# A two-layer attention and expert trunk on one core: paired products, and a branch over the first expert's quads

## The chip, the cores and the metric

The kernel runs on one core of a Trainium2 chip. The core has TensorE (PE, with its weight loads PEld), VectorE (DVE), ScalarE (ACT), GpSimd (POOL) and SyncE (SP), and 16 DMA engines. TensorE runs at one of two clock levels, 1.2 or 2.4 GHz; the profile gives the granted clock as a share of the higher. The metric is the device time of one execution in microseconds, by the median of several runs.

## The reference

256 tokens of width 1024 pass two layers, each an attention and a feed-forward part with a layer norm behind it. Layer 0 has sliding-window attention (16 heads) and a dense SwiGLU of 3584. Layer 1 has attention in three branches (compressed keys and values, selected blocks, window) and eight SwiGLU experts of 3584, of which each token takes two.

```python
def reference(x, ...):
    cos, sin = _rope_tables(x.shape[1])
    for i in range(DEPTH):
        j = i // 2
        if i % 2 == 0:
            h = _swa_sink_attention(x, a_w_in[j], a_w_out[j], a_sinks[j], cos, sin)
        else:
            h = _nsa_attention(x, b_w_in[j], b_w_out[j], b_cmp_pos_k[j], b_cmp_pos_v[j],
                               b_cmp_k_w1[j], b_cmp_k_w2[j], b_cmp_v_w1[j], b_cmp_v_w2[j], cos, sin)
        x = _layer_norm(DN_ALPHA * x + h, ln_gain[i, 0], ln_bias[i, 0])
        if i % 2 == 0:
            f = _swiglu(x, ffn_w_gate[j], ffn_w_up[j], ffn_w_down[j])
        else:
            f = _moe(x, moe_router[j], moe_w_gate[j], moe_w_up[j], moe_w_down[j])
        x = _layer_norm(DN_ALPHA * x + f, ln_gain[i, 1], ln_bias[i, 1])
    return x

# inside _nsa_attention
    def compress(t, pos, w1, w2):
        blk = t[:, idx] + pos[None, None, :, None, :]
        flat = blk.transpose(0, 1, 3, 2, 4).reshape(B, nc, Hkv, CMP_LEN * HEAD_DIM)
        return jax.nn.gelu(flat @ w1) @ w2
    kcc = compress(kc, pos_k, ck_w1, ck_w2)
    vcc = compress(vc, pos_v, cv_w1, cv_w2)

def _moe(x, router, w_gate, w_up, w_down):
    xt = x.reshape(B * S, D)
    logits = (xt @ router).astype(jnp.float32)
    vals, ids = lax.top_k(logits, TOP_K)
    w = jax.nn.softmax(vals, axis=-1)
    gate = jnp.sum(jax.nn.one_hot(ids, N_EXPERTS, dtype=jnp.float32) * w[..., None], axis=1)
    for e in range(N_EXPERTS):
        out = out + gate[:, e:e + 1].astype(xt.dtype) * _swiglu(xt, w_gate[e], w_up[e], w_down[e])
```

## The kernel before

**Stages.** Everything is one unrolled program. `plan` lists the weights in the order of use as tiles of 1 MB (2048 columns of 128 partitions), and `load` asks for them on SP's queue (L168) as soon as a buffer is free: seven `raw` buffers, and in the experts seven `more` and five `later`. The first tile is cut into two pieces. The products of layer 0 and of the projections split each weight tile into `hi` (ACT, L120) and `lo` (DVE, L121) and take three products of 128x512 each (`mm3`, L204 to L206). At the start PE transposes x (L224), ACT and DVE split the transposed tokens into `Th` and `Tl`, and `project` makes the products of token tile 0, then 1.

**Compression.** In `compress` the products of keys and values with `w1` (L803) have 64 columns of PE each: 16 for keys and then 16 for values, both to the same half of the columns (each is two rows in the trace). The sum `hc` is 64 partitions by 512; the gelu (L807 to L815) is a chain of ACT and DVE steps on that shape, then four transposes (L820).

**Attention of layer 1.** `unit(t, j, heads)` does scores, softmax, transposes and value products (L948) of a pair of heads j. For t = 0 both heads are in one unit and the products alternate between the two halves of PE's columns; for t = 1 each head is a unit of its own, with its eight trace rows all in one half. Units are pipelined by `pairs` with one step of each between the products of the last query projection.

**Experts.** Expert 0's gathering (`first_gather`, L1092) is interleaved by hand with the router in a `manual_schedule` of PE, DVE, POOL and ACT. An expert of at most 96 tokens has its first 64 done as *halves* (`halves`, two column halves, L1187 for gate and up, L1210 for down) and the other 32 as *quads* (`quarters`, four column quarters, L1195 and L1216). Expert 0 always has both, as have four other places; three places have 64 only (`CAPS`). `two` does one and then the other and turns the order round each time, so that two groups of the same kind follow each other. An expert has four chunks of 1024, 1024, 1024 and 512, with gate, up and down in each: twelve groups of halves, and twelve of quads. In the experts PE's order is as written. Behind the router, DVE counts and ranks the experts (L1359 to L1366); SP loads seven registers from `whole` (L1381) to know which expert's weights to ask for next, and its queue stands still until it has them. At the end of the program all engines branch over the code for overflowing experts (L1402, L1403).

## Time and profile before

| what | us |
|---|---|
| median of three runs (1411.89 to 1418.05) | 1413.41 |
| the profiled execution | 1413.78 |
| its span | 1412.0 |
| PE busy in the span | 1360.7 (96%) |
| DVE busy | 442.0 (31%) |
| ACT busy | 342.4 (24%) |

The granted clock was 0.99 of the higher level in the mean. The share of PE is high throughout, but PE is busy for two reasons: up to about 530 us because its products are the longest work, and behind that because the experts' products take about as long as the transfer of their weights (434.86 MB in all, 308 GB/s over the span, about 405 in the experts). A row of the timeline gives start and length in us, engine and line, the operation with the tile written and the tiles read, the shape and the count; in brackets stands the idle time before it and who ended it.

### The profile page before, as it was taken

What the parts mean: (1) busy time and instruction counts of PE and PEld (TensorE: products, weight loads), DVE (VectorE), ACT (ScalarE), POOL (GpSimd) and SP (SyncE); (2) the same over time, 40 slices, a digit from 0 to 9 for tenths busy, and PEclk for the clock granted to TensorE, in tenths of its full rate; (3) what the DMA queues carried; (4) which work ended last, traced back from release to release, by engine and by line L of the source; (5) the groups of instructions that cost most, each with busy time, mean ns of one, the idle gap of its engine ahead of it and who ended that gap; (6) DMA issues with size and microseconds to landing.
All of it is one profiled execution on the core that took longest, in us unless ns stands there. A gap on an engine that the chain in (4) does not pass through costs nothing. (4 is left out here: it accounts for less than half of the span.)

```text
span 1412.0 us, 23279 instructions
## 1 busy us (share of the span) xinstructions
PE 1360.7 (96%) x9761; PEld 784.5 (56%) x9762; DVE 442.0 (31%) x1004; ACT 342.4 (24%) x783; POOL 8.4 (1%) x17
## 2 busy tenths in 40 slices
PE   7999999999999999999999999999998999999984
PEld 6777888887777774453344354444343454445331
DVE  6876544556958753000101001100100100200103
ACT  5754444444456721010001001000101000100100
POOL 0000000000000000000000000000000000000000
PEclk9999999999999998999999999999999999999997
DMA  9516565554372067899999999999999999999994
GB/s 349 181 61 211 181 192 192 179 179 155 122 271 91 31 266 272 345 389 377 409 403 409 407 401 409 408 402 407 408 402 409 408 401 408 408 395 393 408 402 179
DMA packets 143679, 434.86 MB, mean 308 GB/s; under 512 B 11312, under 2 KB 18128, under 8 KB 143568
## 3 DMA queue, kind: packets, MB, share of 16 engines
q1 hardware_dynamic: 138416, 428.85, 79.3%
q10 hardware_dynamic: 5152, 4.45, 1.0%
q8 instruction: 79, 1.29, 0.4%
q14 instruction: 32, 0.26, 0.1%
HBM read 432.23 MB, written 1.05 MB: 307 GB/s over the span
## 5 line engine op out<-in xcount | busy, mean ns | idle before, releaser
L121 DVE TENSOR_TENSOR lo<-raw,hi 128x512 fp32r<-128x512 f32 (+2 forms) x244 | 166.4, 730 | 106.5 <-ACT hi L120 106.3
L1187 PE MATMUL ps<-more,Th 128*64 128x512 f32 (+1 forms) x920 | 186.8, 555 | 5.7 <-DMA more<-in_moe_w_gate 5.4
L120 ACT ACTIVATE hi<-raw 128x512 fp32r<-128x512 f32 (+2 forms) x244 | 146.0, 659 | 142.4 <-PE ps L206 129.5
L204 PE MATMUL ps<-hi,Th 128*128 128x512 f32 (+1 forms) x432 | 171.4, 397 | 4.4 <-ACT hi L120 3.2
L206 PE MATMUL ps<-hi,Tl 128*128 128x512 f32 (+1 forms) x432 | 168.6, 391 | 1.4 <-DVE Tl L121 1.4
L205 PE MATMUL ps<-lo,Th 128*128 128x512 f32 (+1 forms) x432 | 168.3, 390 | 0.0
L1244 DVE TENSOR_TENSOR h<-h,ps 128x512 f32<-128x512 f32 (+1 forms) x32 | 19.9, 621 | 448.4 <-PE ps L1187 448.4
L1187 PE MATMUL ps<-later,Th 128*64 128x512 f32 (+1 forms) x680 | 128.9, 525 | 2.1 <-DMA later<-in_moe_w_gate 1.8
L1187 PEld LDWEIGHTS ps<-more,Th 128*64 128x64 f32 x920 | 65.0, 138 | 115.5 <-issue 98.4
L204 PEld LDWEIGHTS ps<-hi,Th 128*128 128x128 f32 x432 | 81.9, 190 | 23.6 <-ACT hi L120 3.6
L1187 PE MATMUL ps<-raw,Th 128*64 128x512 f32 (+1 forms) x448 | 94.4, 561 | 0.6 <-ACT Th L1095 0.6
L1210 PE MATMUL ps<-more,hTa 128*64 128x512 f32 x408 | 92.2, 595 | 2.7 <-DMA more<-in_moe_w_down 2.7
L1236 ACT ACTIVATE h<-ps 128x512 f32<-128x512 f32 (+1 forms) x32 | 17.4, 544 | 315.1 <-PE ps L1187 315.1
L206 PEld LDWEIGHTS ps<-hi,Tl 128*128 128x128 f32 x432 | 81.8, 189 | 20.4 <-DVE Tl L121 2.9
L205 PEld LDWEIGHTS ps<-lo,Th 128*128 128x128 f32 x432 | 82.0, 190 | 16.8 <-DVE lo L121 0.4
L1187 PEld LDWEIGHTS ps<-later,Th 128*64 128x64 f32 x680 | 47.8, 137 | 72.1 <-issue 60.1
L1210 PE MATMUL ps<-later,hTa 128*64 128x512 f32 x312 | 70.3, 594 | 2.0 <-DMA later<-in_moe_w_down 2.0
L1210 PEld LDWEIGHTS ps<-more,hTa 128*64 128x64 f32 x408 | 28.4, 137 | 60.6 <-issue 54.6
L1187 PEld LDWEIGHTS ps<-raw,Th 128*64 128x64 f32 x448 | 31.7, 139 | 53.1 <-issue 48.6
L1195 PE MATMUL ps<-more,Th 128*32 128x256 f32 (+1 forms) x1136 | 60.2, 359 | 0.0
L1239 ACT ACTIVATE hb<-ps 128x256 f32<-128x256 f32 (+1 forms) x20 | 7.2, 358 | 189.0 <-PE ps L1195 189.0
L1243 DVE TENSOR_TENSOR hb<-hb,ps 128x256 f32<-128x256 f32 (+1 forms) x20 | 7.8, 388 | 142.3 <-PE ps L1195 142.3
(256 smaller groups left out, 1444.5 us busy)
## 6 DMA issues: line engine op xcount, KB each, us to landing
more<-in_moe_w_up SPq DMA_DIRECT2D x53, 1024.0 KB, 18.1
more<-in_moe_w_down SPq DMA_DIRECT2D x51, 1024.0 KB, 18.0
more<-in_moe_w_gate SPq DMA_DIRECT2D x50, 1024.0 KB, 18.2
later<-in_moe_w_down SPq DMA_DIRECT2D x38, 1024.0 KB, 15.1
later<-in_moe_w_gate SPq DMA_DIRECT2D x36, 1024.0 KB, 18.3
later<-in_moe_w_up SPq DMA_DIRECT2D x35, 1024.0 KB, 18.0
raw<-in_moe_w_gate SPq DMA_DIRECT2D x26, 1024.0 KB, 18.0
raw<-in_moe_w_up SPq DMA_DIRECT2D x24, 1024.0 KB, 18.2
```

The source lines that it names most:

```text
L120: state["act"] = ACT.activation(hi, src, AF.Copy)
L121: DVE.tensor_tensor(lo, src, hi.bitcast(F32), op=OP.subtract)
L204: PE.matmul(ps, xh, wh, start=first, stop=False)
L205: PE.matmul(ps, xh, wl, start=False, stop=False)
L206: PE.matmul(ps, xl, wh, start=False, stop=last)
L1187: PE.matmul(pa[h * CA:(h + 1) * CA, :wide // 2], T[:, k, :CA], parts[k // n][:, k % n, h * wide // 2:(h + 1) * wide // 2], start=k == 0, s ...
L1195: PE.matmul(pb[q * CB:(q + 1) * CB, :wide // 4].rearrange("p (b f) -> p b f", f=CB), T[:, k, CA:], w[:, q], start=k == 0, stop=k == KT - 1)
L1210: PE.matmul(ya[o * CA:(o + 1) * CA, :], hT[0][:, f % (n // 2), f // (n // 2), :], parts[f // 2][:, f % 2, o * 512:(o + 1) * 512], **ends(f))
L1236: ACT.activation(ha, ga[:, :wide // 2], AF.Silu)
L1239: ACT.activation(hb, gb[:, :wide // 4], AF.Silu)
L1243: DVE.tensor_tensor(hb, hb, ub[:, :wide // 4], op=OP.mult)
L1244: DVE.tensor_tensor(ha, ha, ua[:, :wide // 2], op=OP.mult)
```

## The change

- `zeros` is made first, on DVE, and in a manual schedule PE does seven products with it ahead of the transposes of x and five behind them.
- The first weight tile is cut into four pieces, which are asked for on ACT's queue.
- The tiles of `w1` come in turns for keys and values, and their products go to one half of the columns each, in turns; the gelu runs on 128x256, with two transposes of 128x128.
- The value products of head 0 of token tile 1 are kept and issued with those of head 1, in turns.
- Expert 0 does its halves first each time; a register on PE (`beyond`, the count of expert 0 less 64) decides whether its quads are branched over. The banks that quads would fill are set to zero by DVE. `cnt` and `beyond` are made inside the manual schedule.

The three calls of `gate_up` and `down`, which pass `x`, are left out.

```diff
+    zeros = const.tile([P, P], BF16, name="zeros")
+    DVE.memset(zeros, 0.0)
     cbf = const.tile([P, 3 * P], BF16, name="cbf")
...
             pieces = min(n, pieces if state["loaded"] < len(order) - 2 else 2)
+            queue = ACT if len(order) > 99 and state["loaded"] == 1 else SP
             for k in range(0, n, n // pieces):
-                SP.dma_start(raw[:, k:k + n // pieces, :], src[:, k:k + n // pieces, :])
+                queue.dma_start(raw[:, k:k + n // pieces, :], src[:, k:k + n // pieces, :])
             raws.append((raw, exact, kind))
...
     wa, wo = a["a_w_in"][0], a["a_w_out"][0]
-    plan(wa[:, :512], pieces=2)
+    plan(wa[:, :512], pieces=4)
     for c in (1024, 512):
...
     KC, VC, KS, VS, KW, VW, GL = (1024 + 256 * k for k in range(7))
-    w1s = [a[w][0, q * 1024:(q + 1) * 1024, :] for w in ("b_cmp_k_w1", "b_cmp_v_w1") for q in range(2)]
+    w1s = [a[w][0, q * 1024:(q + 1) * 1024, :] for q in range(2) for w in ("b_cmp_k_w1", "b_cmp_v_w1")]
     plan(wb[:, KC:KC + 512])
...
         with tc.manual_schedule(engines={PE.engine}):
+            idle = bank()
+            def turn_over(n):
+                for _ in range(n):
+                    PE.matmul(idle, zeros, zeros.unsqueeze(1).to_broadcast([P, 4, P]), start=True, stop=True)
+            turn_over(7)
+            Ts[0]
+            turn_over(5)
             for _ in project(Ts, 512, ps_q[0], 2):
...
-    zeros = const.tile([P, P], BF16, name="zeros")
-    POOL.memset(zeros, 0.0)
     SP.dma_start(cmask, a["cmask"].rearrange("(t p) k c -> p t k c", p=P))
...
             DVE.tensor_copy(posT, pb[:, :32].rearrange("p (a b) -> p a b", a=2))
-            hc = bank().rearrange("p (k h) -> p k h", k=2)[:C]
+            hc = bank()[:, :CMP_HID]
             Xs = wts.tile([P, 2, CMP_LEN // 2, NKV, CP], F32, name="X", tag="raw", bufs=RAW)
...
                 yield
-            for k in range(2):
-                for q in range(2):
-                    (r,), = take()
-                    for i in range(8):
-                        PE.matmul(hc[:, k, :], Xs[:, k, q * 8 + i].rearrange("p g c -> p (g c)"), r[:, i, :],
-                                  start=q == 0 and i == 0, stop=q == 1 and i == 7, skip_group_check=True)
+            for q in range(2):
+                r = [w for (w,) in take(2, 1 + q)]
+                for i in range(8):
+                    for k in range(2):
+                        PE.matmul(hc[k * C:(k + 1) * C, :], Xs[:, k, q * 8 + i].rearrange("p g c -> p (g c)"),
+                                  r[k][:, i, :], start=q == 0 and i == 0, stop=q == 1 and i == 7,
+                                  skip_group_check=True)
                 yield
-            hx, hy = (pool.tile([P, 2, CMP_HID], F32, name="hx", tag="pt", bufs=PT)[:C] for _ in range(2))
+            hx, hy = (pool.tile([P, CMP_HID], F32, name="hx", tag="pt", bufs=PT) for _ in range(2))
             ACT.activation(hx, hc, AF.Copy)
...
             yield
-            pb = bank().rearrange("p (k j c) -> p k j c", k=4, j=2)[:, :2, :, :]
-            for k in range(2):
-                for j in range(2):
-                    PE.transpose(pb[:, k, j, :], hx[:, k, j * P:(j + 1) * P], ident[:C, :C])
+            pb = bank()[:, :CMP_HID].rearrange("p (j k c) -> p k j c", j=2, k=2)
+            for j in range(2):
+                PE.transpose(pb[:, :, j, :].rearrange("p k c -> p (k c)"), hx[:, j * P:(j + 1) * P], ident)
...
-        sums = {}
+        sums, waiting = {}, {}
...
             yield
-            if heads[0] == 0:
+            if heads[-1] == 1:
                 sums[t, j] = bank()[:, :P]
-            po = sums[t, j]
-            for m, (i, br, k) in enumerate(steps):
-                h = heads[i]
-                PE.matmul(po[h * HD:(h + 1) * HD, :], v[:, k, br, g, :], pt[:, m * P:(m + 1) * P],
-                          start=k + br == 0, stop=False, skip_group_check=True)
+            po = sums.get((t, j))
+            held = waiting.setdefault((t, j), [])
+            held += [(k, br, heads[i], pt, m) for m, (i, br, k) in enumerate(steps)]
             if heads[-1] == 1:
+                for k, br, h, x, m in sorted(held, key=lambda e: e[:3]):
+                    PE.matmul(po[h * HD:(h + 1) * HD, :], v[:, k, br, g, :], x[:, m * P:(m + 1) * P],
+                              start=k + br == 0, stop=False, skip_group_check=True)
                 PE.matmul(po, vcc[:, j // 4, j % 4].rearrange("p e d -> p (e d)"), pcT[:, t, j // 4, :], start=False,
...
-            self.cap, self.slot, self.gate = cap, slot_e, gate_e
+            self.cap, self.slot, self.gate, self.more, self.ask = cap, slot_e, gate_e, None, None
...
-        def two(first, second, between=None):
+        def two(x, first, second, between=None):
-            steps = [first, second][::-1 if state["turn"] and second else 1]
-            if second:
+            both, ask = second is not None, x.ask is not None
+            steps = [first, second][:1 + both]
+            if both and not ask:
+                if state["turn"]:
+                    steps.reverse()
                 state["turn"] = 1 - state["turn"]
-            steps[0]()
-            if between:
-                between()
-            if second:
-                steps[1]()
+            for i, step in enumerate(steps):
+                if i == 1 and ask:
+                    state["turn"] = 1
+                    x.more = x.ask() if x.more is None else x.more
+                    with tc.If(x.more > 0):
+                        step()
+                else:
+                    step()
+                if i == 0 and between:
+                    between()
-        def gate_up(pa, pb, T, wide):
+        def cleared(ps, x):
+            if x.ask is not None:
+                DVE.memset(ps, 0.0)
+        def gate_up(pa, pb, x, wide):
+            T = x.T
+            if pb is not None:
+                cleared(pb[:, :wide // 4], x)
             parts = [w for (w,) in take(KT * wide // PART, 0)]
...
-            two(halves, pb is not None and quarters)
+            two(x, halves, quarters if pb is not None else None)
-        def down(c, hT, ya, yb, between=None):
+        def down(c, hT, ya, yb, x, between=None):
+            if yb is not None and c == 0:
+                cleared(yb[:, :256], x)
             n = WIDE[c] // P
...
-            two(halves, yb is not None and quarters, between)
+            two(x, halves, quarters if yb is not None else None, between)
...
     mvs = {}
+    cnt = moe.tile([P, NE], F32, name="cnt")
+    beyond = moe.tile([P, 1], I32, name="beyond")
     with tc.manual_schedule(engines={PE.engine, DVE.engine, POOL.engine, ACT.engine}):
...
         next(gathering)
+        ps = bank()[:, :NE]
+        for t in range(NT):
+            PE.matmul(ps, ones, asb[:, t, :], start=t == 0, stop=t == NT - 1)
+        DVE.tensor_copy(cnt, ps)
+        DVE.tensor_scalar(beyond, cnt[:, 0:1], -float(CA), 0.0, op0=OP.add, op1=OP.max)
         for _ in share():
             pass
+    experts[0].ask = lambda: nc.values_load(beyond[0:1, :], engines=[PE.engine], min_val=0, max_val=S)
     halves_pool.__exit__(None, None, None)
...
-    ps = bank()
-    for t in range(NT):
-        PE.matmul(ps[:, :NE], ones, asb[:, t, :], start=t == 0, stop=t == NT - 1)
-    NR = NE - 1
-    cnt, key, rank = (moe.tile([P, NE], F32, name=x) for x in ("cnt", "key", "rank"))
+    key, rank = (moe.tile([P, NE], F32, name=x) for x in ("key", "rank"))
     is_at = moe.tile([P, NE, NE], F32, name="is_at")
...
-    DVE.tensor_copy(cnt, ps[:, :NE])
     DVE.scalar_tensor_tensor(key, cnt, float(NE), iota8, op0=OP.mult, op1=OP.add)
```

The first place is PE in the attention of layer 1: L948 is the value products, L951 the compressed part, L939 transposes, L920 scores. Before, around the second unit of a pair with t = 1:

```order
L948 MATMUL ps<-pt,v 64x128 x4
L206 MATMUL ps<-hi,Tl 128x512
L939 MATMUL ps<-cf,p 128x128 x4
L917 LDWEIGHTS cbf
L917 MATMUL ps<-masks,cbf 128x512
L920 MATMUL ps<-kT,qT_2938 128x256 x4
L948 MATMUL ps<-pt,v 64x128 x4
L951 MATMUL ps<-pcT,vcc 128x128
```

After, where L963 is L948:

```order
L210 MATMUL ps<-hi,Tl 128x512
L951 MATMUL ps<-cf,p 128x128 x4
L929 LDWEIGHTS cbf
L929 MATMUL ps<-masks,cbf 128x512
L932 MATMUL ps<-kT,qT_2955 128x256 x4
L963 MATMUL ps<-pt,v 64x128 x8
L965 MATMUL ps<-pcT,vcc 128x128
```

The first head's products no longer stand with the mask and scores ahead, and eight program rows for both heads stand where the second head's four stood.

The second place is PE at the first expert: L1092 is the gathering, L1187 halves, L1195 quads. Before:

```order
L1092 MATMUL ps<-pick,x_80 128x96 x4
L1187 MATMUL ps<-raw,Th 64x512
L1092 MATMUL ps<-pick,x_80 128x96 x4
L1187 MATMUL ps<-raw,Th 64x512 x15
L1195 MATMUL ps<-raw,Th 32x256 x56
L1195 MATMUL ps<-more,Th 32x256 x8
L1187 MATMUL ps<-raw,Th 64x512 x12
```

After, where L1106 is the gathering, L1218 halves, L1226 quads and L1365 the register:

```order
L1106 MATMUL ps<-pick,x_82 128x96 x8
L1360 LDWEIGHTS cbf
L1360 MATMUL ps<-asb,cbf 128x8
L1360 LDWEIGHTS cbf
L1360 MATMUL ps<-asb,cbf 128x8
L1218 MATMUL ps<-raw,Th 64x512 x16
L1365 TENSOR_LOAD beyond
L1365 ISA x2
L1196 COMPARE_AND_BRANCH
L1226 MATMUL ps<-raw,Th 32x256 x32
L1196 UNCONDITIONAL_BRANCH x2
L1218 MATMUL ps<-raw,Th 64x512 x12
```

All eight gathering products stand ahead of the first halves, the count's products (L1360) follow them, and each group of quads stands between a branch that compares and two that don't.

The third place is DVE behind the router: `w2t` is the softmax of the two choices, `whole` the ranked experts. Before:

```order
L1362 TENSOR_TENSOR tmp<-key 128x64
L1363 TENSOR_REDUCE rank<-tmp 128x8
L1364 TENSOR_TENSOR is_at<-cf,rank 128x64
L1356 TENSOR_TENSOR tmp<-is_at,cf 128x64
L1357 TENSOR_REDUCE numbers<-tmp 128x8
L1366 CAST whole<-numbers 128x8
L1356 TENSOR_TENSOR tmp<-is_at,slot 128x64
L1357 TENSOR_REDUCE slots<-tmp 128x8
L1356 TENSOR_TENSOR tmp<-is_at,slot 128x64
L1075 TENSOR_SCALAR pick<-cf,slots 128x64
L1357 TENSOR_REDUCE slots<-tmp 128x8
L1044 TENSOR_SCALAR w2t<-w2t 128x2
```

After, just behind the first step on `w2t` (L1058):

```order
L1399 TENSOR_TENSOR tmp<-key 128x64
L1059 RECIPROCAL w2t<-w2t 128x2
L1400 TENSOR_REDUCE rank<-tmp 128x8
L1061 TENSOR_TENSOR w2t<-w2t 128x2
L1062 TENSOR_TENSOR hot<-hot,w2t 128x2x8
L1401 TENSOR_TENSOR is_at<-cf,rank 128x64
L1064 TENSOR_TENSOR hot<-hot,w2t 128x2x8
L1394 TENSOR_TENSOR tmp<-is_at,cf 128x64
L1066 TENSOR_TENSOR hot<-hot 128x2x8
L1395 TENSOR_REDUCE numbers<-tmp 128x8
L1068 CAST gates<-hot 128x16
L1403 CAST whole<-numbers 128x8
```

The cast to `whole` stood ahead of the first step on `w2t` behind ACT; now six steps on `w2t`, `hot` and `gates` stand between the ranking's and ahead of the cast. On SP the register loads of `whole` then stand behind one more weight tile. Before:

```order
L168 DMA more<-in_moe_w_gate 128x2x1024 x4
L168 DMA more<-in_moe_w_up 128x2x1024
L168 DMA later<-in_moe_w_up 128x2x1024
L168 DMA more<-in_moe_w_up 128x2x1024
L1381 TENSOR_LOAD whole
L1381 ISA x2
```

After:

```order
L172 DMA more<-in_moe_w_up 128x2x1024
L172 DMA later<-in_moe_w_up 128x2x1024
L172 DMA more<-in_moe_w_up 128x2x1024
L172 DMA later<-in_moe_w_up 128x2x1024
L1418 TENSOR_LOAD whole
L1418 ISA x2
```

The second `later` tile of `in_moe_w_up` has come ahead of the loads.

## Rows read from the trace of the kernel before

**Rows 1.** The page's 40 slices of the span: bandwidth of the transfers in each.

```profile
GB/s 349 181 61 211 181 192 192 179 179 155 122 271 91 31 266 272 345 389 377 409 403 409 407 401 409 408 402 407 408 402 409 408 401 408 408 395 393 408 402 179
```

**Rows 2.** Timeline of SyncE's queue: start, length, instruction, count.

```profile
506.90 0.37 SPq L168 DMA_DIRECT2D more<-in_moe_w_up  x1
...
537.54 0.38 SPq L168 DMA_DIRECT2D later<-in_moe_w_up  x1
```

**Rows 3.** Timeline of TensorE and ScalarE at the start; idle time before in brackets.

```profile
9.39 0.79 PE L204 MATMUL ps<-hi,Th 128*128 128x512 f32 x1 [3.21 <-ACT hi L120]
...
14.13 0.47 PE L205 MATMUL ps<-lo,Th 128*128 128x512 f32 x1
...
17.24 0.39 PE L206 MATMUL ps<-hi,Tl 128*128 128x512 f32 x1
...
12.77 1.15 ACT L120 ACTIVATE hi<-raw 128x512 fp32r<-128x512 f32 x2 [0.19 <-DMA raw<-in_a_w_in]
```

**Rows 4.** Timeline of TensorE: the compression.

```profile
398.81 7.12 PE L803 MATMUL ps<-raw,X 128*64 128x256 f32 x32
...
421.87 0.65 PE L391 MATMUL ps<-cf,kd 128*128 128x128 f32 x4 [2.80 <-ACT kd L120]
```

**Rows 5.** Timeline of TensorE: value products of layer 1.

```profile
442.68 1.09 PE L948 MATMUL ps<-pt,v 128*64 128x128 f32 x8
...
447.71 0.66 PE L948 MATMUL ps<-pt,v 128*64 128x128 f32 x8
```

**Rows 6.** Timeline of VectorE: the gelu of the compression.

```profile
410.30 3.34 DVE L814 RECIPROCAL hx<-hx 64x512 f32<-64x512 f32 x1
```

**Rows 7.** Windows of 10 us: busy time and count by engine, granted clock, DMA, GB/s.

```profile
410.00:420.00 10.00, 9.07 (x70) 8.62 (x69) 9.99 (x20) 6.60 (x16) 0.00 (x0) 1.00 0.68 239
...
450.00:460.00 10.00, 9.43 (x68) 7.70 (x69) 8.36 (x29) 9.12 (x33) 0.00 (x0) 1.00 0.00 1
```

**Rows 8.** Timeline of TensorE: one group of quads of the first expert.

```profile
566.00 3.66 PE L1195 MATMUL ps<-more,Th 128*32 128x256 f32 x64
```

**Rows 9.** Windows of 4 us, columns as in rows 7: the first expert.

```profile
528.00:532.00 4.00, 2.78 (x17) 2.37 (x16) 3.49 (x17) 0.15 (x1) 0.00 (x0) 0.71 0.42 166
532.00:536.00 4.00, 3.61 (x10) 2.00 (x10) 1.53 (x9) 1.28 (x2) 0.00 (x0) 0.50 0.81 262
536.00:540.00 4.00, 4.00 (x12) 1.31 (x13) 2.80 (x19) 1.86 (x3) 0.00 (x0) 0.51 0.31 69
...
556.00:560.00 4.00, 4.00 (x22) 1.40 (x20) 0.69 (x1) 0.00 (x0) 0.00 (x0) 1.00 0.35 138
560.00:564.00 4.00, 4.00 (x22) 1.33 (x20) 0.00 (x0) 0.00 (x0) 0.00 (x0) 1.00 0.77 262
564.00:568.00 4.00, 4.00 (x50) 1.66 (x50) 0.00 (x0) 0.60 (x1) 0.00 (x0) 1.00 0.00 0
568.00:572.00 4.00, 4.00 (x72) 2.30 (x68) 0.00 (x0) 0.98 (x2) 0.00 (x0) 1.00 0.90 320
...
644.00:648.00 4.00, 4.00 (x50) 1.76 (x50) 0.00 (x0) 0.00 (x0) 0.00 (x0) 1.00 0.67 265
648.00:652.00 4.00, 4.00 (x41) 1.57 (x34) 0.00 (x0) 0.00 (x0) 0.00 (x0) 1.00 0.76 255
```

**Rows 10.** Timeline of VectorE after the router.

```profile
532.59 0.17 DVE L1366 CAST whole<-numbers 128x8 int32<-128x8 f32 x1
...
536.96 0.17 DVE L1044 TENSOR_SCALAR w2t<-w2t 128x2 f32<-128x2 f32 x1 [3.26 <-ACT w2t L1042]
```

**Rows 11.** Line 1403, the branch over the overflow: ns min/median/max, first and last start.

```profile
L1403 ACTq EVENT_SEMAPHORE  x2: 17/17/17, 1395.9 to 1396.0; - x2
...
L1403 ACTq COMPARE_BRANCH  x1: 45/45/45, 1395.6 to 1395.6; - x1
L1403 PEldq COMPARE_BRANCH  x1: 3394/3394/3394, 1397.9 to 1397.9; - x1
```

**Rows 12.** Waits of SyncE's queue: total us, times, longest us.

```profile
SPq L1403 <- SPq L1403: 11.5, 6, 5.2
```

More of the change, by code (lines that the diff above doesn't have):

```diff
@@ L1231, in run_experts @@
                 ga, gb = bank(), bank() if rest else None
-                gate_up(ga, gb, x.T, wide)
+                gate_up(ga, gb, x, wide)
                 finish()
@@ L1240, in run_experts @@
                 ua, ub = bank(), bank() if rest else None
-                gate_up(ua, ub, x.T, wide)
+                gate_up(ua, ub, x, wide)
                 if rest:
@@ L1265, in back @@
                 def back(between=None, c=c, hT=hT, ys=ys, x=x):
-                    down(c, hT, *ys, between)
+                    down(c, hT, *ys, x, between)
                     if c == len(WIDE) - 1:
```

## The prediction

> **What bounds the kernel now.** I read the page's slices first, then windows and timelines of the stretches that the change touches. The slices have two regimes [rows 1]. Up to the 15th slice (about 530 us) the transfers run at 31 to 349 GB/s while TensorE has almost no idle time: there TensorE sets the pace, and what it saves moves everything behind it. From the 17th slice on they run at about 405 GB/s: the experts' weights are 1 MB tiles of 2.6 us (1.05 MB over 408 GB/s), and the time is set by transfers that come late. So a saving ahead of 506 us, where the first tile of the stage's larger buffers is asked for [rows 2], should arrive whole at the end; in the experts only holes in the transfers can be closed. The sum is made against the profiled execution, 1413.78 us (span 1412.0), which is 0.4 us over the median of the three runs.
>
> **Start.** The first real product waits until 9.39 for the halves of the first weights and runs at half clock: ten products from 9.39 to 14.13 are 0.47 apart, thirteen from 14.13 to 17.24 0.24 apart [rows 3]. The zero products (12 of 0.47 at most, so 5.7 us) fill TensorE's wait; the seven ahead of the transposes could delay them, and the five behind would then be late too, by 2 us at most. If the clock is high by the first product, the products no longer set the end of this block; the weights do. ACT splits the last piece from 12.77 [rows 3], DVE follows, and the last products can end about 14 instead of 17.6, a gain of 3.3. Pieces of half the size land a little earlier; but the first weights now ask on ACT's queue beside x, which the transposes need, and may push it back by half a microsecond. I take 2.6, between 0 (clock not raised in time) and 3.3.
>
> **Compress.** Two groups of 32 products of 7.12 us each run alone in one half of the columns [rows 4]. In pairs the two column halves work at once. What that gives is shown in the attention of this trace: eight value products of one head take 1.09 us, eight that alternate between two heads' halves 0.66 [rows 5], and as the last product's tail of some 0.25 is in both, the pitch halves (0.12 to 0.06). So 7.1 us go. The chain of the gelu works on 128x256 rather than 64x512: its reciprocal of 3.34 us [rows 6] becomes about 1.7, and the other six vector steps lose some 1.2 in all. Behind it TensorE idles 2.80 us for kd [rows 4], at the end of a stretch in which DVE is busy 9.99 of 10 us [rows 7]; I give 2.0 of the 2.8 back, by DVE's relief of 2.9. Compress: 9.1, between 7.1 and 9.9. The sixteen transposes between the groups stay where they are.
>
> **Value products.** For the second token tile each head's eight run alone; afterwards two heads' sixteen alternate. Per pair 16 x 0.12 becomes 16 x 0.06, 0.97 us, and with eight pairs 7.8 at most. In this stretch ACT is busy 9.12 and DVE 8.36 of 10 us in the densest window, TensorE 9.43 [rows 7], so with TensorE 12% faster the others come close. Head 0's pt is held longer, and its products queue behind head 1's. I take 5.5, between 0 and 7.8.
>
> **Quads branched over.** From the reference's own formulas on its inputs, expert 0 gets 60 tokens, so the branch over the quads is taken, twelve times. A full group of 64 quad products takes 3.66 us [rows 8], nine such and three of half the length about 36 us in all, 3.0 a group. Against that each group pays a branch and a drain of TensorE: c. This is worth something only where transfers wait for buffers. Against 408 GB/s the windows lose 7.1 us from 528 to 540, 8.9 from 556 to 572 and 2.9 from 644 to 652 [rows 9]. The second and third (11.8) are buffers that the expert's products free late; these close when TensorE runs 3.0 - c faster per group. The first is the router's: SP's register loads wait for `whole`, ready at 532.59, and the next tile goes out at 537.54 [rows 2, 10]. Now `whole` stands behind the steps on w2t, the first of which waits for ACT until 536.96 [rows 10], about 0.9 ahead of the new cast: 537.9 instead of 532.6, so SP resumes 5.3 later. One tile more is ordered ahead of the loads, 2.6 us of transfer; the first hole grows by 2.7. Eight gather products ahead of the first halves instead of four delay TensorE by 1.9, which the closed holes absorb.
>
> c is what this trace doesn't show for such a jump. At the end every engine jumps over the overflow code: ACT's branch at 1395.6 (45 ns) is followed by the next semaphore at 1395.9, with some 80 instructions passed over; TensorE's takes 3.39 us, with over 700; SP, with some 240, stands 5.2 us at most behind its own [rows 11, 12]. A group of quads is 128 instructions in the trace (64 weight loads and 64 products), nearer to ACT's. I take c = 0.7: 0.3 for the jump and 0.4 for the drain. Its ends are 0.3 and 5.2. About three groups run ahead of the second hole, so up to c = 3.0 each microsecond of c costs three; beyond, all twelve groups are slower than the quads were, and it costs twelve. The experts: -11.8 + 2.7 + 3 x 0.7 = -7.0.
>
> The Trainium skill ("Runtime: NRT & Kernel Launch", section "Instruction fetch mechanics") says that a taken branch to a target outside the two instruction pages at hand stalls for a fetch. TensorE's 3.39 us agrees; ACT's 0.3 is a jump without it. By the page's 256 instructions a page, a jump of 128 mostly stays inside, which as an estimate gives the forecast; with every jump fetched, rival 1 holds.
>
> The clearing memsets on DVE and the branches on the four other engines (45 ns on ACT [rows 11]) lie beside engines that idle in this stretch; I cost them at nothing.
>
> **Sum.** 2.6 + 9.1 + 5.5 + 7.0 = 24.2: 1413.8 - 24.2 = 1389.6, less the 0.4 to the median 1389.2; I say 1389.5.
>
> **Rivals.**
> 1. The jump over the quads costs what TensorE's own did. With c = 3.4: -11.8 + 2.7 + 9.0 + 12 x 0.4 = +4.7; with the 17.2 of the other three parts 1401. For it speaks that it is the only TensorE branch in the trace; against it that it was five times as far. Between c of 1.5 and 4.4: 1392 to 1413. Chance 0.16.
> 2. Slower: the refill of TensorE's instructions queues among the weight transfers, which leave no gap at 405 GB/s, as SP's 5.2 may have. At c = 5.2: -0.1 + 12 x 2.2 = +26, and 1422. It decides from c = 4.4, where 12 x 1.4 eats the 17.2. The bubbles could add a lower clock. Chance 0.07.
> 3. The earlier gains are absorbed: DVE and ACT set the pace in attention (0 to 2 left), the clock rises too late (0 to 1), compress gives its 7.1. Then 9 + 7.0 leave 1397 or 1398. For it: ACT at 9.12 of 10. Against: TensorE's idle time in front of the value products is all but nil. Chance 0.16.
> 4. The change doesn't skip: expert 0 has more than 64 tokens on the chip. Then the quads run, twelve drains come on top and the holes stay: +2 to +7 in the experts, 1398 to 1403. Chance 0.05.
>
> **How the numbers follow.** The forecast has 0.56. Faster by over 0.5% (7 us, what a measurement of this kernel can tell from no change) means below 1406: forecast 0.56, rival 3 0.16, 0.13 of rival 1, 0.04 of rival 4, so 0.89. Slower by over 0.5% is rival 2 but for its beginning, 0.06; 0.05 is left between. The range: at the low end all three early parts whole (3.3 + 9.9 + 7.8) and c = 0.3, with one more microsecond of closed holes: 21.0 + 9.2 = 30.2, 1383; I go to 1381, since the small holes further on may close too. At the high end rivals 1, 3 and 4 up to 1403.
>
> **What would show it.** Right: last products of the first block at 14 to 15 us; L803's successor two groups of about 3.6 us and no idle of 2.8 for kd; value products of 16 in about 1.1 us; the first `more` tile asked for at about 490 instead of 506.9; in expert 0 no quads, halves following each other within 1 us; after the hole at the router no window under 380 GB/s until the experts' end. Wrong: gaps of 2 us or more at each branch of TensorE, DVE or ACT near 10 of 10 in attention with TensorE idle, or quads in the trace of expert 0.

## The result, and the profile after

The changed kernel takes 1380.32 us (median of four runs, 1379.07 to 1381.95) against 1413.95 of before beside it: a ratio of 0.976, interval 0.9735 to 0.9784, 33.6 us less. The forecast was 1389.5 in a range of 1381 to 1403. The sign held, and so did three of the four parts; but the gain was 33.6 where the sum had 24.2, and the time lies 0.7 us under the low end, which is less than the four runs differ among themselves.

The profiled execution has a span of 1378.8 us. Its slices answer to [rows 1]: the two low ones (13th and 14th) are still there, but a rate of 400 is reached in the 17th slice and not in the 20th: the slices of 345, 389 and 377 are gone.

```profile
GB/s 354 189 62 213 184 185 183 183 183 183 115 268 120 62 296 370 400 409 409 402 409 408 402 408 409 403 406 403 407 403 409 408 401 408 407 393 393 408 402 160
```

To see where the time went, read the same events in both traces; the distance between two events, before less after, is what that stretch gave. The tiles qs and kd are transposed ahead of the compression and behind it. These are rows of the timelines of TensorE and SyncE in the changed kernel, against [rows 2, 4] and the events of the same name:

```profile
387.53 1.03 PE L395 MATMUL ps<-cf,qs 128*128 128x128 f32 x8
388.49 3.67 PE L815 MATMUL ps<-raw,X 128*64 128x256 f32 x32
393.99 3.67 PE L815 MATMUL ps<-raw,X 128*64 128x256 f32 x32
410.22 0.66 PE L395 MATMUL ps<-cf,kd 128*128 128x128 f32 x4
...
486.29 0.37 SPq L172 DMA_DIRECT2D more<-in_moe_w_up  x1
```

| from, to | before | after | gain | forecast |
|---|---|---|---|---|
| start, transposes of qs ahead of the compression | 388.89 | 387.53 | 1.4 | 2.6 |
| those, first transposes of kd | 32.98 | 22.69 | 10.3 | 9.1 |
| those, first `more` tile asked for | 85.03 | 76.07 | 9.0 | 5.5 |
| that, end of the span | 905.1 | 892.5 | 12.6 | 7.0 |

The pairs of the compression do halve (7.12 to 3.67), and the 2.80 us of idle time ahead of kd are gone. In the value products sixteen now take as long as eight did in [rows 5], while VectorE and ScalarE are busier than in the second window of [rows 7]. A row of the timeline of TensorE, and a window with the columns of rows 7:

```profile
432.38 1.09 PE L963 MATMUL ps<-pt,v 128*64 128x128 f32 x16
433.40 0.49 PE L965 MATMUL ps<-pcT,vcc 128*128 128x128 f32 x2
```

```profile
430.00:440.00 10.00, 9.02 (x76) 7.21 (x75) 9.43 (x31) 9.21 (x32) 0.00 (x0) 1.00 0.21 84
```

In the first expert the windows that answer to [rows 9] show the hole at the router still there, and no second one:

```profile
508.00:512.00 4.00, 2.60 (x22) 2.20 (x22) 2.87 (x10) 1.19 (x2) 0.00 (x0) 1.00 0.27 105
512.00:516.00 4.00, 4.00 (x22) 1.51 (x23) 3.47 (x29) 2.23 (x4) 0.00 (x0) 1.00 0.95 330
516.00:520.00 4.00, 3.84 (x20) 1.21 (x18) 3.52 (x20) 0.68 (x2) 0.00 (x0) 1.00 0.50 201
520.00:524.00 4.00, 4.00 (x22) 1.61 (x20) 0.53 (x4) 0.19 (x1) 0.00 (x0) 1.00 0.81 289
...
536.00:540.00 4.00, 4.00 (x22) 1.39 (x20) 0.00 (x0) 0.00 (x0) 0.00 (x0) 1.00 1.02 410
548.00:552.00 4.00, 3.70 (x19) 1.26 (x17) 0.00 (x0) 0.00 (x0) 0.00 (x0) 1.00 1.03 411
...
624.00:628.00 4.00, 4.00 (x22) 2.41 (x20) 2.48 (x4) 1.20 (x2) 0.00 (x0) 1.00 1.03 411
```

Against 408 GB/s the first four lose 6.9 us (7.1 before); in the last three, which stand where before the second and third hole stood (8.9 and 2.9), nothing is lost. The branch line (duration in ns, minimum, median and maximum, first and last start) and the halves behind two of the branches:

```profile
L1196 PEldq COMPARE_BRANCH  x12: 207/236/1213, 516.3 to 612.4; - x12
```

```profile
519.43 5.37 PE L1218 MATMUL ps<-raw,Th 128*64 128x512 f32 x24 [0.16 <-PEq L1196]
...
526.82 7.09 PE L1218 MATMUL ps<-more,Th 128*64 128x512 f32 x32 [0.30 <-PEq L1196]
```

The twelve branches are taken, and TensorE idles 0.14 to 0.31 us behind eleven of them (behind the last it waits 0.71 us for weights).

### The profile page after: what moved, and what is told of

Same layout as the page of the kernel before. It is cut to its first block, busy times and chain, and to the rows that moved or that the text cites. A ratio compares the mean times of both kernels' runs of the same rounds, so it can differ in the third digit from the quotient of the medians.

```text
span 1378.8 us, 21888 instructions
## 1 busy us (share of the span) xinstructions
PE 1315.0 (95%) x9035; PEld 751.4 (54%) x9036; DVE 441.4 (32%) x1015; ACT 342.9 (25%) x783; POOL 8.2 (1%) x16
## 5 line engine op out<-in xcount | busy, mean ns | idle before, releaser
L1218 PE MATMUL ps<-more,Th 128*64 128x512 f32 (+1 forms) x920 | 187.3, 555 | 6.4 <-DMA more<-in_moe_w_gate 3.4
L1218 PE MATMUL ps<-later,Th 128*64 128x512 f32 (+1 forms) x680 | 129.1, 525 | 4.7 <-DMA later<-in_moe_w_up 3.5
L1218 PEld LDWEIGHTS ps<-more,Th 128*64 128x64 f32 x920 | 65.2, 138 | 116.5 <-issue 94.0
L1218 PE MATMUL ps<-raw,Th 128*64 128x512 f32 (+1 forms) x448 | 91.1, 550 | 3.0 <-DMA raw<-in_moe_w_gate 2.5
L209 PEld LDWEIGHTS ps<-lo,Th 128*128 128x128 f32 x432 | 81.7, 189 | 16.4 <-issue 0.2
L1218 PEld LDWEIGHTS ps<-later,Th 128*64 128x64 f32 x680 | 47.3, 137 | 76.0 <-issue 58.8
L1218 PEld LDWEIGHTS ps<-raw,Th 128*64 128x64 f32 x448 | 31.4, 137 | 55.3 <-issue 44.4
L1226 PE MATMUL ps<-more,Th 128*32 128x256 f32 (+1 forms) x928 | 49.8, 361 | 4.5 <-DMA more<-in_moe_w_gate 4.5
L1243 PEld LDWEIGHTS ps<-later,hTa 128*64 128x64 f32 x312 | 22.2, 137 | 49.5 <-issue 41.2
```

What stands on the lines that cost most here:

```text
L209: PE.matmul(ps, xh, wl, start=False, stop=False)
L1218: PE.matmul(pa[h * CA:(h + 1) * CA, :wide // 2], T[:, k, :CA], parts[k // n][:, k % n, h * wide // 2:(h + 1) * wide // 2], start=k == 0, s ...
L1226: PE.matmul(pb[q * CB:(q + 1) * CB, :wide // 4].rearrange("p (b f) -> p b f", f=CB), T[:, k, CA:], w[:, q], start=k == 0, stop=k == KT - 1)
L1243: PE.matmul(ya[o * CA:(o + 1) * CA, :], hT[0][:, f % (n // 2), f // (n // 2), :], parts[f // 2][:, f % 2, o * 512:(o + 1) * 512], **ends(f))
```

## Experiments

Two theories stand against each other for the largest part. A: the experts' gain is the holes in the transfers behind the first halves, closed because expert 0's products take some 37 us less. B: it comes from the new order behind the router, or from TensorE's clock, which fell there before ([rows 9], 0.50) and did not in the profile after. Of the timed kernels each stood beside runs of the kernel before on the same chip.

### The quads done, without a branch

```diff
-    experts[0].ask = lambda: nc.values_load(beyond[0:1, :], engines=[PE.engine], min_val=0, max_val=S)
```

> The changed kernel, with expert 0's quads always done and no branch; the count and the gathering stay where the change put them. Theory A (the experts' gain is the holes behind the first halves, closed because expert 0's products take 72 us and not 108): the windows of 556 to 572 and 644 to 652 of before come back, and the time rises by 11 to 13 us, to about 1392. Theory B (the gain comes from the order behind the router and from a clock that did not fall there, not from the quads): it stays within 4 us of 1380.

With this line gone expert 0's groups also go back to the turned order of before, and no banks are cleared.

Measured: 1391.99 us (1390.18 to 1392.42), 11.7 over the changed kernel. The holes behind the first halves are back, in windows of the same columns:

```profile
540.00:544.00 4.00, 4.00 (x36) 1.42 (x36) 0.00 (x0) 0.60 (x1) 0.00 (x0) 1.00 0.74 294
544.00:548.00 4.00, 4.00 (x72) 2.30 (x68) 0.00 (x0) 0.98 (x2) 0.00 (x0) 1.00 0.69 215
...
624.00:628.00 4.00, 4.00 (x56) 1.91 (x50) 0.00 (x0) 0.00 (x0) 0.00 (x0) 1.00 0.51 148
```

Theory A. The gathering stood first here too, so the order alone gives next to nothing: from the first `more` tile to the end this kernel takes 903.3 us, before 905.1. The holes are not the same ones to the microsecond. Only one tile of the pair that the change has ahead of the register loads goes out there in this kernel, so the hole at the router (508 to 524) loses 10.3 us (its four windows carry 140, 266, 0 and 172 GB/s), and those behind it lose less than before: against 408 GB/s the windows from 44 to 164 us behind the first `more` tile lose 8.8 us here, 14.6 before and 0.4 in the changed kernel.

### The experts' part alone, and the other three alone

The first is the diff with its parts on start, compression and value products taken back, the second with those on the experts taken back.

> The kernel before, with the experts' part of the change alone (count, branch, cleared banks). Theory A: the same 12 to 13 us as in the whole change, so about 1401. Theory B: the first expert's stretch depends on where TensorE's clock falls, which the earlier parts moved; then less than 8 us, 1406 or more, with a stretch of half clock at the first expert.

> The changed kernel without the experts' part: start, compress and value products alone. Theory A: the shift of the first tile of the larger buffers, 20.6 us (506.90 to 486.29), arrives whole at the end: 1414 - 20.6 = 1393. Theory B: some of it is lost or won behind the router; then the time lies 4 us or more away from that.

Measured: 1403.01 us (1402.05 to 1409.63) and 1394.23 (1388.62 to 1395.15), beside 1413.16 of before: 10.2 and 18.9, of which the first is under the expected 12 to 13 and lies between the two theories, and the second is theory A within 1.2. Together they make 29.1 of the 33.6, and the rest is within the spread of the runs. The profile, which was the slowest of the five runs of the first kernel, gives the better measure, the stretch from the first `more` tile (513.36) to the end (1407.8): 894.4 us, near the 892.5 of the whole change. TensorE ran at half clock behind the router here too, which was theory B's condition, and the gain stayed; so theory A. In the second kernel the same stretch takes 905.6 us, as before (905.1). That the first profile is 6.5 us late at 513.36 has its cause ahead of the edit: TensorE's idle time for kd, which this kernel still has, was followed by some 17 us of half clock. Windows of 5 us, and the row of kd's transposes:

```profile
420.00:425.00 5.00, 3.63 (x18) 3.56 (x18) 3.65 (x6) 4.32 (x10) 0.00 (x0) 0.56 0.34 137
425.00:430.00 5.00, 5.00 (x22) 4.61 (x21) 2.74 (x7) 0.82 (x2) 0.00 (x0) 0.50 0.64 210
430.00:435.00 5.00, 5.00 (x18) 4.51 (x19) 3.44 (x12) 0.76 (x3) 0.00 (x0) 0.50 0.48 157
435.00:440.00 5.00, 5.00 (x19) 3.49 (x18) 1.83 (x4) 1.17 (x5) 0.00 (x0) 0.73 0.13 52
```

```profile
421.37 3.68 PE L391 MATMUL ps<-cf,kd 128*128 128x128 f32 x16 [2.80 <-ACT kd L120]
```

The stretch from kd to the first `more` tile took 92.0 us in it, and 85.0 in the first profile of before, which has the same 2.80 us without a fall (the third profile with it, of the old compression below, has a short one: 0.90 and 0.76 from 415 to 425). So the value of closing that gap differs from run to run.

### One part undone at a time

Each of the three early parts was taken back from the diff by itself, beside the changed kernel itself once more.

> The changed kernel itself once more, as the reference for the three kernels beside it: 1380 us, with the first tile of the larger buffers asked for at 486 us. Where TensorE's granted clock falls to half may differ from the first profile.

> The changed kernel with the value products issued head by head as before. Theory A (TensorE alone sets the pace there): between kd's transposes and the first tile of the larger buffers 8.9 us come back, 8.2 as eight groups of 1.02 us and the rest as a wait for pt; time 1389. Theory B, as in the prediction (DVE and ACT take part of the gain): 5.5 us, 1386.

> The changed kernel with the compression as before. Theory A: 7.1 us of products and the idle time of 2.8 us for kd come back, 10 us, time 1390; in some executions the idle time may also let the clock fall, which adds up to 6 us. Theory B: the chain of the gelu is hidden anyway, only the 7.1 us of products come back, 1387.

> The changed kernel with the start as before: no zero products, the first weights in two pieces on SP's queue. Theory A, by the trace of the changed kernel (1.4 to 1.7 us ahead at 17 us and at 388 us): the first tile of the larger buffers is asked for 1.4 to 1.7 us later and the time rises by as much, 1382. Theory B, the prediction's 2.6 or more: 1383 to 1384.

Measured: 1381.79 (1380.25 to 1382.86), 1390.75 (1390.74 to 1393.41), 1391.42 (1390.63 to 1392.45) and 1381.17 (1380.11 to 1381.48). So the value products are worth 9.0 us, the compression 9.6, and the start nothing that these runs can tell. The profiles say it stretch by stretch. Of the kernel with the old value products, kd's transposes and the first `more` tile:

```profile
408.74 0.66 PE L395 MATMUL ps<-cf,kd 128*128 128x128 f32 x4
...
493.76 0.37 SPq L172 DMA_DIRECT2D more<-in_moe_w_up  x1
```

That is 85.02, against 76.07 and 76.08 in the two profiles of the change: 8.9, theory A. (That the times differ by as much is partly luck: in the profile this kernel is 1.7 us ahead at kd, and it takes 1.9 us more behind the first `more` tile, since one tile fewer stands ahead of the register loads.) Of the kernel with the old compression:

```profile
386.36 1.03 PE L395 MATMUL ps<-cf,qs 128*128 128x128 f32 x8
...
419.34 3.42 PE L395 MATMUL ps<-cf,kd 128*128 128x128 f32 x16 [2.80 <-ACT kd L122]
```

From qs to kd 32.98, as before to the hundredth, and 22.69 in both profiles of the change: 10.3, theory A. (Some 0.5 of that is two products of the projection that now stand behind kd and not ahead.) With the old start the first `more` tile goes out at 486.44, with the new one at 486.29 and 486.55: neither theory, nothing.

### The start without the zero products

```diff
-            turn_over(7)
             Ts[0]
-            turn_over(5)
```

> The changed kernel without the zero products, the early weights on ACT's queue kept. If the zero products make the start's gain, the first block runs at half clock to about 14 us and its last product ends near 17.6 as before; if the early weights make it, it ends 1 us earlier. In the profiles so far the clock fell again between 5 and 65 us in four of seven kernels with zero products and in none of three without; here it should not fall there.

One execution: 1382.11 us. The rows of its first product, of the first of those that follow each other every 0.24 us or less, and of the transposes of x1, the second token tile:

```profile
7.35 0.79 PE L208 MATMUL ps<-hi,Th 128*128 128x512 f32 x1
...
10.31 0.40 PE L210 MATMUL ps<-hi,Tl 128*128 128x512 f32 x1
...
14.72 1.04 PE L228 MATMUL ps<-cf,x 128*128 128x128 f32 x8
```

Without zero products the first real one starts at 7.35 (8.66 and 7.98 in the two profiles with them), the short spacing begins at 10.31 (10.65 and, but for one product, 8.40 with them), and x1's transposes stand at 14.72, between the 14.03 and 15.32 of the two profiles with them. So what was won at this point (17.47 before, 16.18 in the changed kernel with the old start) came with the early weights, 1.5 to 2.8 us where 1 was expected, and the zero products cost about what they give. The other expectation missed: the clock did fall between 50 and 65 us here, so that fall does not need them. One execution decides little below 1.5 us; the falls of the clock in the first 65 us come and go from run to run.

### No branch and no quads

```diff
-                    x.more = x.ask() if x.more is None else x.more
-                    with tc.If(x.more > 0):
-                        step()
+                    pass
```

> The changed kernel with expert 0's quads left out when the program is built, and neither register nor branch (it would miss tokens if expert 0 had more than 64). Theory A: the branches cost TensorE 12 x 0.3 = 3.6 us, but in a stretch where it waits for transfers anyway, so the time is that of the change within 1 us, 1380. Theory B: the drain at each branch delays buffers; then 3 to 4 us faster, 1377.

Measured: 1380.61 us (1379.44 to 1382.59). The halves run on where the branches stood:

```profile
512.15 12.24 PE L1216 MATMUL ps<-raw,Th 128*64 128x512 f32 x56
```

Theory A: TensorE saves the gaps and gives them back as waits for weights, which from 508 to 640 us grow from 8.0 to 10.6 us. The branch costs nothing that can be measured here.

### Longer blocks to branch over

```diff
                     with tc.If(x.more > 0):
-                        step()
+                        for _ in range(4):
+                            step()
```

and the same with 16.

> The changed kernel with each branched-over block four times as long (the group of quads written four times in it, never run; 512 instructions a block in place of 128). Theory A (a jump is cheap while its target is among the instructions already at hand): this one is near or past the edge, and some of the twelve jumps cost 1 to 4 us where the short ones leave TensorE idle for 0.31 at most. Theory B (a taken branch costs the same at any distance, and the 3.39 us at the program's end has another cause): 0.3 us each, time unchanged at 1380.

> The same with blocks sixteen times as long (2048 instructions). Theory A: every jump costs 2.4 to 5 us; at 3.4 us each of the twelve that is 41 us against the 36 of the quads, so the gain in the experts is gone and the time is about 1395 to 1400. Theory B: 0.3 us each, 1380.

One execution each: 1395.35 and 1397.44 us. Line 1196 of the first and of the second, and of the first the products behind three branches and behind one other stop:

```profile
L1196 PEldq COMPARE_BRANCH  x12: 348/6080/6814, 519.1 to 642.2; - x12
```

```profile
L1196 PEldq COMPARE_BRANCH  x12: 3517/6062/6914, 520.2 to 642.5; - x12
```

```profile
531.98 7.09 PE L1219 MATMUL ps<-more,Th 128*64 128x512 f32 x32 [2.01 <-PEq L1196]
...
551.20 5.03 PE L1244 MATMUL ps<-later,hTa 128*64 128x512 f32 x14 [2.69 <-PEq L1196]
...
597.40 6.45 PE L1127 MATMUL ps<-pick,x 128*128 128x64 f32 x30 [5.26 <-issue]
...
619.49 3.33 PE L1244 MATMUL ps<-raw,hTa 128*64 128x512 f32 x8 [4.55 <-PEq L1196]
```

Theory A, and more sharply than expected: at 512 instructions the branch takes 6.1 us in the median where the short one takes 0.24, and at 2048 it takes no more. TensorE, which still has halves queued when the branch begins, idles up to 4.6 us of it. The whole gain in the experts is gone at that price: from the first `more` tile to the end these kernels take 907.0 and 908.7 us, with the quads done 903.3. Not all of it is the branch itself. Both kernels stop once more for 5.2 us two products behind a branch, with no releaser shown, and both run part of the stretch at half clock (in the first 0.50 from 596 to 608 us). Nothing of these blocks runs; they are only passed over. The pages show what goes with the dear branches: the packets of the instruction queue, in the changed kernel, with blocks of four and with blocks of sixteen:

```profile
q8 instruction: 79, 1.29, 0.4%
```

```profile
q8 instruction: 94, 1.54, 0.5%
```

```profile
q8 instruction: 95, 1.56, 0.5%
```

Fifteen or sixteen packets of 16 KB more are fetched for twelve longer blocks, and about as many for 2048 instructions as for 512, so their number goes with the branches and not with what is passed over. That a branch stands still for such a packet fits this; which branch waited for which packet is not shown.

### The experts' numbers loaded later

```diff
-    who = {0: 0}
+    who = Lazy(lambda e: nc.values_load(whole[0:1, 0, e:e + 1], engines=[SP.engine], min_val=0, max_val=NE - 1))
...
-    for e in range(1, NE):
-        who[e] = nc.values_load(whole[0:1, 0, e:e + 1], engines=[SP.engine], min_val=0, max_val=NE - 1)
```

`Lazy` loads a number when it is first asked for.

> The changed kernel, with the seven register loads of the experts' numbers taken out of SP's way: each number is loaded where the first tile of that expert is asked for. If the hole at the router (6.9 us lost from 508 to 524) is SP standing behind the loads, three more tiles of 2.6 us go out about 8 us earlier, the hole closes to about 1 us and the time falls by 5 to 7 us, to about 1374. If the buffers are what is missing then (raw buffers that the first halves free from 515 on), the hole moves and less than 3 us are won.

Measured: 1378.45 us (1376.55 to 1380.05). SyncE goes on at once, and one window of the hole is left:

```profile
510.94 1.89 SPq L172 DMA_DIRECT2D later<-in_moe_w_down  x3
518.34 0.37 SPq L172 DMA_DIRECT2D raw<-in_moe_w_down  x1
```

```profile
508.00:512.00 4.00, 3.12 (x23) 2.38 (x24) 2.76 (x11) 2.08 (x4) 0.00 (x0) 1.00 0.28 55
512.00:516.00 4.00, 4.00 (x22) 1.40 (x20) 3.82 (x29) 1.33 (x2) 0.00 (x0) 1.00 1.00 403
516.00:520.00 4.00, 3.84 (x20) 1.22 (x18) 3.06 (x16) 0.87 (x2) 0.00 (x0) 1.00 1.02 409
```

The hole shrinks from 6.9 to 3.5 us, and from the first `more` tile to the end the profile has 889.6 us and not 892.5. The expected 5 to 7 us did not come, since the loads are only half of the hole: the other half lies ahead of them, where SyncE's queue waits 7.7 us until the tile before goes out at 510.00. It is the fastest kernel of this study by its median, but its ratio to before is the same (0.9756 against 0.9759, with intervals that nearly coincide): the 3 us are seen in the trace, and the runs do not separate them from the change.

## Why the prediction fell short, and what was right in it

The gain in the profiles is 33.2 us (1412.0 less 1378.8) and the sum was 24.2. By the table the 9 us are 5.6 in the experts, 3.5 in the value products and 1.2 in the compression, less 1.2 at the start.

**Start.** Forecast 2.6, found 1.4 in the first profile and nothing in the runs. The step that failed is that the end of the first block sets the gain. In the first profile the last products ended at 15.5, and not at about 14; in the second they ended at 14.2, and TensorE then idled 1.97 us. Three rows of the first profile and one of the second:

```profile
5.53 0.63 PE L228 MATMUL ps<-cf,x 128*128 128x128 f32 x4 [1.50 <-DMA x<-in_x]
6.52 0.66 PE L228 MATMUL ps<-cf,x 128*128 128x128 f32 x4 [0.36 <-DMA x<-in_x]
...
17.04 0.50 PE L208 MATMUL ps<-hi,Th 128*128 128x512 f32 x1 [0.69 <-ACT Th L122]
```

```profile
17.04 0.50 PE L208 MATMUL ps<-hi,Th 128*128 128x512 f32 x1 [1.97 <-ACT Th L122]
```

The next block begins at 17.04 in both (17.02 without zero products, 17.46 with the old start), because x1's tokens wait for ScalarE, which splits the next weights from 14.31 to 16.4. That wait was not in the sum. The weights also pushed x back further than the half microsecond allowed for: its transposes began at 5.53 and 6.52, not at 4.24. At qs the 1.4 is no more than what the mark moves by itself, 386.04 to 389.05 in ten profiles with the new start and 387.64 to 388.89 in three with the old one. That a fall of the clock shortly after takes back the rest is possible; no run isolates it.

**Compression.** Right in mechanism; 10.3 for 9.1. All of the 2.8 us of idle time went, not 2.0 of it, and about half a microsecond is work that moved past the mark.

**Value products.** Forecast 5.5 with a bound of 7.8, measured 8.9. Two steps failed. The deduction for VectorE and ScalarE was wrong: they went to 9.43 and 9.21 of 10 us, but TensorE waited for VectorE's p 1.0 us in all, where before it waited 0.8 us for ScalarE's pt. That is rival 3, and it did not happen. And the bound was too low: the price of a group was taken as 8 x 0.12, but a group holds TensorE for 1.02 us (from 442.68 in [rows 5] to the next instruction), which makes 8.2 for eight. In the kernel before:

```profile
443.70 0.50 PE L206 MATMUL ps<-hi,Tl 128*128 128x512 f32 x1
```

The last 0.7 may be the 0.1 by which this product behind such a group is late (0.34 to the next and not 0.23); that was only read, not tested.

**Quads.** The skip held, so expert 0 had at most 64 tokens, and so did the closing of the 11.8 us of holes. Two terms were mis-sized. c, the price of a branch to its group, was 0.3 where 0.7 was taken, and its price of 3 us for each microsecond is nil as long as TensorE is ahead of the transfers: without any branch the time is the same. That is 2.1. And the first hole didn't grow by 2.7; it lost 6.9 instead of 7.1. The row for w2t [rows 10] was read as the time at which ScalarE can deliver. It was the time at which ScalarE got round to it, behind an evacuation of the second gathering, which stood behind the first halves at half clock. In the kernel before, 0.4 us ahead of that step on w2t:

```profile
536.35 0.49 ACT L1095 ACTIVATE Th<-ps 128x384 f32<-128x384 f32 x1 [3.06 <-PE ps L1092]
```

With the gathering ahead, w2t is there 0.8 us after the count and `whole` 2.2 us after it, and SyncE's next tile goes out 4.96 us behind `whole` (4.95 before):

```profile
512.30 0.17 DVE L1361 COPY cnt<-ps 128x8 f32<-128x8 f32 x1 [0.94 <-PE ps L1360]
...
513.14 0.17 DVE L1058 TENSOR_SCALAR w2t<-w2t 128x2 f32<-128x2 f32 x1
...
514.53 0.17 DVE L1403 CAST whole<-numbers 128x8 int32<-128x8 f32 x1
```

```profile
519.49 1.40 SPq L172 DMA_DIRECT2D later<-in_moe_w_down  x3
```

Counted from the first `more` tile, `whole` comes at 28.2 us and came at 25.7: 2.6 us later and not 5.3, which the one tile more ahead of the loads (2.6 us) just covers. In the two profiles with the skip where that tile did not go ahead (the experts' part alone, the old value products) the first hole lost about 10 us.

With those two terms corrected the experts' sum is about 12, and the profiles differ by 11.4 in the mean (three without the skip take 903.3 to 905.6 us from the first `more` tile to the end, seven with it 891.9 to 895.2). TensorE's clock fell to half for some us behind the router in all three without the skip and in six of the seven with it, so the clock is not what makes this gain.

**Rivals.** 1 and 2 (a dear jump) did not happen at this length, and the runs with longer blocks show that a dear jump is real: with 512 instructions the change would have been rival 1. Rival 4 is excluded, since no quads of expert 0 ran. The Trainium skill ("Runtime: NRT & Kernel Launch", section "Instruction fetch mechanics"), with its stall for a target that is not at hand, agrees with 0.24 us at 128 instructions and 6.1 at 512, and with the packets fetched for the longer blocks; the edge between them was not looked for.

**The range** ended at the sum of all the bounds, and three of its terms were themselves too small: 7.8 for the value products (8.9), 9.9 for the compression (10.3), and the grown hole, which had no range of its own.

**Readings.** Four readings in the prediction were off, and none decides the result. From 17.6 to 14 is 3.6 and not 3.3. The half clock of the first products was read from their spacing; the granted clock of the windows from 8 to 16 us is 1.00 in the profile of before. The rate of about 405 holds from the 20th slice on; the three slices before it have 345, 389 and 377. And nine groups of quads of 3.66 us with three of half the length make 38 us and not 36 (some 37 from group to group).

## What to carry to other kernels

Price a skipped group by what waits for it: here some 37 us of products were worth 11 to 12, the holes in the transfers behind them, and the branches nothing, as TensorE had time to spare. Keep what is branched over short: here the same branch over four times the code took 1395.35 us, and doing the work 1391.99. When a row is used as the time at which an input can be had, look at what its engine did just before: a late start may be only its place in the queue, and the edit moves that too.

## What was not expected of the hardware

A branch over 128 instructions takes 0.24 us on TensorE's queue (median; 1.2 at most) and one over 512 takes 6.1, with weights moving at up to 415 GB/s; the branch at the end of the kernel before, with 3 GB/s moving, took 3.39 over a longer way. Whether the weights beside it make the difference between 3.39 and 6.1 was not tested. TensorE's granted clock falls at different places in executions of the same code: a wait of 2.80 us was followed by half clock in one profile and not in another, and behind the router the changed kernel kept the high clock in its first profile and ran at half clock in its second:

```profile
510.00:515.00 5.00, 5.00 (x22) 4.10 (x24) 2.62 (x13) 2.59 (x5) 0.00 (x0) 0.50 0.53 158
```

It cost little there: the stretch from the first `more` tile to the end took 893.4 and not 892.5 us.
